# Roots of three group norms and attention's inverse denominators spread to all partitions through DRAM instead of by transposes on TensorE

## The chip, the cores and the metric

One core of a Trainium2 chip runs the whole program. The metric is the device time of one execution in microseconds (us), the median of several runs. The profile is that of one further execution. PE is TensorE, DVE VectorE, ACT ScalarE, POOL GpSimd; SP is SyncE, which only issues DMAs here.

## What is computed

One layer of a decoder trunk on 512 tokens of width 1024, in float32: an RMS norm, one large input projection, attention with dilated windows and a state-space branch (SSD, Mamba-2) side by side, a gated sum of both, an output projection, and a SwiGLU network. The two places of the change are the norm over each of four groups of 512 channels of the SSD branch, and the division by the softmax denominators of attention:

```python
# SSD branch: y (512 tokens, 2048), four groups of 512 channels
yg = (y * silu(z)).reshape(b, s, 4, 512)
yg = yg * rsqrt(mean(yg * yg, axis=-1, keepdims=True) + EPS)
# attention: per token and head, over three dilation groups
o = einsum('znhqk,znkhd->znqhd', p, vw) / den
attn = sum(softmax(lses) * outs)            # 8 heads of 64
```

## The kernel before

Tiles hold 128 channels on the partitions and the 512 tokens along the free dimension. Each weight chunk is a block of 1024 rows by 128 columns (512 KB, `wraw`), loaded by SP. ACT writes its upper part `whi` (L81) and DVE the rest `wlo` (L82), in a format with fewer bits, and PE takes three products per 128 rows: `whi` and `wlo` with the upper part of the data, `whi` with its lower part (`project`, L238; a chunk is 24 products of 512 columns). Each of `wraw`, `whi` and `wlo` has three buffers; loads run two chunks ahead and splits one.

Work of other kinds is threaded between the projections. `hook` (L223) is called in the middle and at the end of each projection; it runs what stands in `late`, moves each generator in `quick` on to its next `yield`, and at a projection's end moves the first generator in `slow` on. After that a scheduler orders the instructions of each engine; each engine then works through its own list in order, and waits where an instruction's semaphore is not there yet. In the SSD part PE, DVE and ACT are ordered by that scheduler too.

The SSD part goes through 16 blocks of 128 channels, four to a group. Each block takes two projections: one through a convolution (`acc`, `th`, `xf`, L525) and one for the gate `zs` (L676). `pair` (L547) then makes the block's decays `a` and `ce`, its states `S`, and `y`, with PE products of 64 rows (a with `xtm`, `ce` with `S`). After a group's last block, `group_end` (L601) takes sums of squares on PE, brings them to the power -1/2 on POOL (`gnr`, L273: token p of each 128 on partition p, four columns), and spreads them: `spread` (L283) transposes each column, repeated 128 times, against the identity on PE (four transposes, L182), so that every partition has the roots of all 512 tokens in PSUM. ACT copies them to `gnb` (L606), DVE multiplies the four `yg` by them (L610) and `split` makes `ssmh` and `ssml` (L258, L259). The second projection of these blocks (`ssm_half`, L617) takes blocks 0 to 7 in the first half, after the third group's blocks, and 8 to 15 much later.

Attention runs in four pairs of heads (`softmax_pair`, L717), each a generator in `slow`, its steps spread over the six projections that follow the pair's own. Small per-token numbers (maxima, `d0`, `d1n`) change their order of tokens by a trip through DRAM issued by POOL (L759 to L764, L781, L783). In the last step PE multiplies the exponentials with the values (`o0`, `o1`, 64-row products). `rd` (L814, L815) is the inverse denominator per token and head; POOL repeats it 64 times (L817), PE transposes that in four pieces into the PSUM bank `pr` (L820), and DVE multiplies the sum `t` of `o0` and `o1` by it (L824), after which `split` makes `ath` and `atl`, from which the merge (L925) takes its products.

Of the kernel before, what the change touches and what calls it, by code (L numbers as in the profile page):

```python
# [9 lines left out]
F32 = mybir.dt.float32  # L10
F32R = mybir.dt.float32r
AF = mybir.ActivationFunctionType
ALU = mybir.AluOpType

P = 128
S = 512
D = 1024
KD = D // P
NCH = S // P
# [149 lines left out]
def trunk(ctx: ExitStack, tc: tile.TileContext, xT, w_in, w_v, w_dt, w_attn, w_ssm, w_out, w_fi, w_fo,  # L169
          prm_d, relb_d, ident_d, tri_d, sid_d, oneh_d, outT, dbg=None):  # L170
    nc = tc.nc
    ev, act, gp, pe = nc.vector, nc.scalar, nc.gpsimd, nc.tensor

    def dump(name, t):
        if dbg and name in dbg:
            nc.gpsimd.dma_start(dbg[name], t)
# [4 lines left out]
    def turn(out, src):  # L181
        pe.transpose(out, src, ident)  # L182
# [10 lines left out]
    drm = ctx.enter_context(tc.tile_pool(name="drm", bufs=1, space=bass.MemoryType.DRAM))  # L193
# [3 lines left out]
    def bank(tag="aux"):  # L197
        cnt[0] += 1
        return psp.tile([P, S], F32, tag=tag, name=f"{tag}{cnt[0]}", bufs=4)
# [7 lines left out]
    def par(name, i=0, w=1):  # L207
        a = PRM[name][0]
        return prm[:, a + i : a + i + w]
# [44 lines left out]
    def split(pool, src, tag, i, tags=None):  # L254

        hi = pool.tile([P, S], F32R, tag=f"{tag}h{i}", name=f"{tag}h{i}_{cnt[0]}")
        lo = pool.tile([P, S], F32R, tag=f"{tag}l{i}", name=f"{tag}l{i}_{cnt[0]}")
        act.activation(hi, src, AF.Copy)  # L258
        ev.tensor_sub(lo, src, hi)  # L259
        return hi, lo  # L260

    def square_sums(ps, sq, first, last):

        for tt in range(sq.shape[1] // P):
            mm(ps[:, tt * 64 : tt * 64 + 64], sq[:, tt * P : tt * P + P], ones[:, :64], start=first and tt == 0, stop=last)

    def inv_root(pool, ps, nt, n, eps, tag):

        cnt[0] += 1
        v = pool.tile([P, NCH], F32, tag=f"{tag}v", name=f"{tag}v{cnt[0]}")[:, :nt]  # L270
        ev.tensor_scalar(v, ps[:, 0 : nt * 64 : 64], 1.0 / n, eps, op0=ALU.mult, op1=ALU.add)
        r = pool.tile([P, NCH], F32, tag=f"{tag}r", name=f"{tag}r{cnt[0]}")[:, :nt]
        gp.tensor_tensor(r, v, mhalf[:, :nt], ALU.pow)  # L273
        return r

    def mean_pow(pool, parts, n, eps, tag):

        ps = bank()
        for i, sq in enumerate(parts):
            square_sums(ps, sq, i == 0, i == len(parts) - 1)  # L280
        return inv_root(pool, ps, parts[0].shape[1] // P, n, eps, tag)

    def spread(r):  # L283

        pb = bank()
        for tt in range(r.shape[1]):
            turn(pb[:, tt * P : tt * P + P], r[:, tt : tt + 1].to_broadcast([P, P]))
        return pb
# [48 lines left out]
    dt, la, te, eE = [ssc.tile([P, P], F32, name=n) for n in ("dt", "la", "te", "eE")]  # L337
    relw = [drm.tile([HEADS, LREL[g]], F32, name=f"relw{g}") for g in range(3)]
    la_d = drm.tile([NSH, S], F32, name="la_d")
    h1_d = drm.tile([P, KD, S], F32, name="h1_d")  # L340
    v_d = [drm.tile([S, S], F32, name=f"v_d{g}") for g in range(3)]
    v_t = [v.rearrange("(c p) d -> p c d", p=P) for v in v_d]
# [6 lines left out]
    with tc.tile_pool(name="s0", bufs=1, reuse_waits="tile") as s0:  # L349
# [7 lines left out]
        v, ab, e, ri, ss, s2, h, dta = [s0.tile([P, P], F32, name=f"c{i}") for i in range(8)]  # L357
# [180 lines left out]
    with tc.tile_pool(name="sp", bufs=1, reuse_waits="tile") as sp:  # L538
# [8 lines left out]
        def pair(t, g, Bt, Cf, cbm, lab):  # L547
# [50 lines left out]
            if t % 4 == 3:  # L598
                quick[1].append(group_end(g))

        def group_end(g):  # L601
            r = mean_pow(sp, [yg.pop((g, "s"))], 512, 4.0 * EPS, "gn")
            yield
            pb = spread(r)
            rb = sp.tile([P, S], F32, tag="gnb", name=f"gnb{g}")
            act.activation(rb, pb, AF.Copy)  # L606
            yield
            for t in range(4 * g, 4 * g + 4):
                y = yg.pop(t)
                ev.scalar_tensor_tensor(y, y, par("nsw", t), rb, op0=ALU.mult, op1=ALU.mult)  # L610
                dump(f"ssm{t}", y)
                cnt[0] += 1
                ssm[t] = split(holder["ssm"], y, "ssm", t % 8)
                if t % 2:
                    yield
# [32 lines left out]
        for g in range(NG):  # L648
# [16 lines left out]
            for p in range(4):  # L665
                t = 4 * g + p
# [31 lines left out]
    attn = [None] * 4  # L698
    mscr = [drm.tile([S, 2], F32, name=f"mscr{i}") for i in range(4)]
    nscr = [drm.tile([S, 2], F32, name=f"nscr{i}") for i in range(4)]  # L700
    dscr = [drm.tile([S, 2], F32, name=f"dscr{i}") for i in range(4)]
    ahl_cm = tc.tile_pool(name="ahl", bufs=1, reuse_waits="tile", side="right")

    with tc.tile_pool(name="ap", bufs=1, reuse_waits="tile") as ap:

        def tl(shape, tag, name, bufs):
            return ap.tile(shape, F32, tag=tag, name=name, bufs=bufs)
# [9 lines left out]
        def softmax_pair(hp, q, k):  # L717
# [14 lines left out]
            for e in range(2):  # L732
                L0, T0 = Ls[e][0], Ts[e][0]
                pa, pb = bank(), bank()
# [78 lines left out]
            rd = tl([P, NCH, 2], "rd", f"rd_{hp}", 2)  # L813
            ev.tensor_add(rd, d0, d1n)  # L814
            ev.reciprocal(rd, rd)  # L815
            rdw = tl([P, NCH, P], "ot", f"rdw_{hp}", 2)
            gp.tensor_copy(rdw.rearrange("p b (e d) -> p b e d", e=2), rd.unsqueeze(3).to_broadcast([P, NCH, 2, 64]))  # L817
            pr = bank()
            for b in range(4):
                turn(pr[:, b * P : b * P + P], rdw[:, b])  # L820
            t = tl([P, S], "ot", f"ot{hp}", 2)
            act.activation(perm(t), regular(o1), AF.Copy)
            ev.tensor_add(t, t, o0)
            ev.tensor_mul(t, t, pr)  # L824
            dump(f"attn{hp}", t)
            attn[hp] = split(holder["ahl"], t, "at", hp)
            yield

        def ttr(out, ps, T, m):
            ev.tensor_tensor_reduce(out, ps, T, 1.0, -3.0e38, op0=ALU.add, op1=ALU.max, accum_out=m)  # L830
# [24 lines left out]
        halves = [slice(e * 64, e * 64 + 64) for e in range(2)]  # L855
# [43 lines left out]
        for hp in range(4):  # L899
            q, k = [], []  # L900
            for g in range(3):
                ps = project(bank("mm"), xn)
                q.append(class_queries(hp, g, ps) if g else first_queries(hp, ps))
                ps = project(bank("mm"), xn)
                k.append(class_keys(g, ps) if g else first_keys(hp, ps))
            slow.append(softmax_pair(hp, q, k))


        for j in range(KD):
            ps = project(bank("mm"), xn)  # L910
            t = tl([P, S], "ot", f"g1_{j}", 2)
# [42 lines left out]
    for i, j in enumerate(OUT_ORDER):  # L954
        t = tmp.tile([P, S], F32, tag="t", name=f"h1_{j}", bufs=2)
# [6 lines left out]
        p = j % 4  # L962
# [104 lines left out]
    for n in range(NF):  # L1067
# [7 lines left out]
        r, q, c1, c5 = heads.pop(n)  # L1075
# [5 lines left out]
        g = fp.tile([P, S], F32, tag="g", name=f"g{n}", bufs=2)  # L1081
# [46 lines left out]
    for j in range(KD - 1):  # L1128
# [6 lines left out]
        t = h1[j]  # L1135
# [175 lines left out]
```

## Time and profile before

| | |
|---|---|
| runs | 1148.74, 1148.74, 1149.55 us; median 1148.74 |
| the profiled execution | 1150.79 us |
| its span, from the first to the last instruction | 1149.0 us |
| mean granted clock of TensorE | 0.996 |
| SSD part, from the first to the fourth group's end | about 60 to 410 us |
| attention pairs | about 500 to 680 us |

In the rows below, times are in us and durations "mean ns of one" in ns. A row of the timeline reads: start, duration, engine, line, operation, output<-inputs, shapes, count, and in brackets the engine's idle time before it and what ended it. A row of waits reads: who waited, for whom, total us, times, longest. `mm` are the PSUM banks of the projections, `aux` those of all else; `PEld` is the loading of PE's stationary operand. In the list of DMA issues the last column is the median time from issue to landing. One `ce` with `S` or `a` with `xtm` counts as two instructions in the trace.

### The profile page before, as it was taken

Reading aid. Unit: us, or ns where it says so; the run is one execution under the profiler, and the core shown is the slowest. Engines: PE = TensorE matmul, PEld = TensorE weight load, DVE = VectorE, ACT = ScalarE, POOL = GpSimd, SP = SyncE. Lnnn points to the kernel's source line nnn. Section 1 sums busy time; section 2 is a strip of 40 time slices with the busy share of each in tenths; the row PEclk is TensorE's granted clock in tenths of the full one; section 3 lists DMA queues with packets and bytes.
Section 4 is the critical chain, followed back from the end, with each engine's and each line's share of the span. In section 5 each row is a group of like instructions: output and inputs, shape, how many; then the busy total and the mean of one; then the engine's idle time right before and its main releaser. Section 6 shows DMA issues by size and latency. Waiting matters only on the chain.

```text
span 1149.0 us, 17104 instructions
## 1 busy us (share of the span) xinstructions
PE 1132.8 (99%) x6636; PEld 969.5 (84%) x6636; DVE 715.3 (62%) x1253; ACT 569.9 (50%) x997; POOL 181.6 (16%) x169
## 2 busy tenths in 40 slices
PE   9999999999999999999999999999999999999996
PEld 6777888878888788888888888888999999988886
DVE  5777897873579333455564534478888777773222
ACT  5555565554345331336536533356767667663321
POOL 3214313222013300011211100000111111100001
PEclk9999999999999999999999999999999999999999
DMA  6343333233332373332333224345688888844322
GB/s 220 130 149 98 121 94 111 92 111 110 92 92 74 110 256 96 106 93 75 93 85 83 63 90 123 112 151 171 148 184 186 191 193 186 172 129 129 101 65 74
DMA packets 51521, 142.35 MB, mean 124 GB/s; under 512 B 6439, under 2 KB 13119, under 8 KB 51184
## 3 DMA queue, kind: packets, MB, share of 16 engines
q1 hardware_dynamic: 42096, 120.90, 33.9%
q0 software_dynamic: 6896, 16.04, 8.4%
q10 hardware_dynamic: 2448, 4.32, 1.3%
q8 instruction: 52, 0.85, 0.3%
q14 instruction: 29, 0.24, 0.1%
HBM read 133.76 MB, written 7.48 MB: 123 GB/s over the span
## 4 chain that ended last, share of the span: by engine, by line
PE 91%; DVE 4%; DMA 2%; ACT 1%; issue 1%; POOL 0%; SPq 0%; ACTq 0%; DVEq 0%; POOLq 0%
PE mm L179 74%; PE aux L179 15%; PE aux L182 2%; DVE wlo L82 1%; DMA x<-xT 0%; DMA lab<-la_d 0%; DVE frl L950 0%; DMA h_d<-h 0%; ACT whi L81 0%; DVE fS_lo L138 0%; DMA fa<-w_fi 0%; DVE xm L469 0%; DVE h L958 0%; POOL n2r L273 0%; DVE fA_lo L131 0%
## 5 line engine op out<-in xcount | busy, mean ns | idle before, releaser
L82 DVE TENSOR_TENSOR wlo<-wraw,whi 128x1024 fp32r<-128x1024 f32 (+2 forms) x156 | 185.7, 1195 | 185.3 <-ACT whi L81 185.1
L81 ACT ACTIVATE whi<-wraw 128x1024 fp32r<-128x1024 f32 (+2 forms) x156 | 152.2, 981 | 267.1 <-PE mm L179 238.1
L179 PE MATMUL mm<-xnh,whi 128*128 128x512 f32 x640 | 251.8, 393 | 1.4 <-DVE acc L530 1.3
L179 PE MATMUL mm<-xnh,wlo 128*128 128x512 f32 x640 | 252.6, 395 | 0.0
L179 PE MATMUL mm<-xnl,whi 128*128 128x512 f32 x640 | 251.1, 392 | 0.0
L179 PEld LDWEIGHTS mm<-xnh,whi 128*128 128x128 f32 x640 | 120.3, 188 | 27.3 <-ACT ce L562 1.7
L179 PEld LDWEIGHTS mm<-xnh,wlo 128*128 128x128 f32 x640 | 120.2, 188 | 26.9 <-issue 2.7
L179 PEld LDWEIGHTS mm<-xnl,whi 128*128 128x128 f32 x640 | 120.2, 188 | 24.9 <-issue 1.2
L179 PE MATMUL mm<-hhl,whi 128*128 128x512 f32 (+1 forms) x171 | 62.6, 366 | 0.6 <-DVE hhl L259 0.6
L179 PE MATMUL mm<-hhh,whi 128*128 128x512 f32 (+1 forms) x171 | 62.8, 368 | 0.2 <-ACT hhh L258 0.2
L179 PE MATMUL mm<-hhh,wlo 128*128 128x512 f32 (+1 forms) x171 | 62.3, 365 | 0.0
L121 POOL DMA_DIRECT2D fD_lo<-w_fi x22 | 19.1, 866 | 246.3 <-DVE h L958 135.8
L563 POOL TENSOR_TENSOR ce<-ce,Cf 128x768 f32<-128x768 f32 x16 | 34.7, 2173 | 140.9 <-ACT ce L562 78.2
L530 DVE SCALAR_TENSOR_TENSOR acc<-mm,hcw,acc 128x511 f32<-128x511 f32 (+2 forms) x72 | 53.2, 743 | 1.0
L138 DVE TENSOR_TENSOR fS_lo<-s,fS_hi 128x1024 fp32r<-128x1024 f32 x44 | 52.0, 1217 | 0.0
L179 PE MATMUL mm<-ssml,whi 128*128 128x512 f32 x128 | 50.2, 392 | 0.0
L179 PE MATMUL mm<-ssmh,wlo 128*128 128x512 f32 x128 | 50.1, 392 | 0.0
L179 PE MATMUL mm<-ssmh,whi 128*128 128x512 f32 x128 | 49.9, 390 | 0.0
L179 PE MATMUL mm<-frh,fS_hi 128*128 128x256 f32 x176 | 49.4, 281 | 0.5 <-ACT c L1031 0.5
L179 PE MATMUL aux<-frh,fS_hi 128*128 128x256 f32 x176 | 49.4, 280 | 0.0
L179 PE MATMUL aux<-frl,fS_hi 128*128 128x256 f32 x176 | 49.1, 279 | 0.0
L179 PE MATMUL aux<-frh,fS_lo 128*128 128x256 f32 x176 | 49.1, 279 | 0.0
(320 smaller groups left out, 2571.1 us busy)
## 6 DMA issues: line engine op xcount, KB each, us to landing
wraw<-w_in SPq DMA_DIRECT2D x80, 512.0 KB, 3.6
fb<-w_fi SPq DMA_DIRECT2D x22, 512.0 KB, 3.7
fa<-w_fi SPq DMA_DIRECT2D x22, 512.0 KB, 5.0
fA_lo<-w_fi POOLq DMA_DIRECT2D x19, 512.0 KB, 5.8
lab<-la_d SPq DMA_DIRECT2D x16, 512.0 KB, 3.7
wraw<-w_ssm SPq DMA_DIRECT2D x16, 512.0 KB, 3.8
wraw<-w_fo SPq DMA_DIRECT2D x15, 512.0 KB, 3.6
wraw<-w_v SPq DMA_DIRECT2D x11, 512.0 KB, 3.7
```

What stands on the lines that cost most here:

```text
L81: self.nc.scalar.activation(hi[:, cs], r[:, cs], AF.Copy)
L82: self.nc.vector.tensor_sub(lo[:, cs], r[:, cs], hi[:, cs])
L121: self.nc.gpsimd.dma_start(lo.rearrange("p (k n) -> p k n", n=P), src, accum_op=ALU.add)
L138: self.nc.vector.tensor_sub(lo, t, hi)
L179: pe.matmul(out, lhsT, rhs, start=start, stop=stop, skip_group_check=True)
L182: pe.transpose(out, src, ident)
L530: ev.scalar_tensor_tensor(acc[:, d:], ps[:, : S - d], hcw[:, t * 4 + 3 - d : t * 4 + 4 - d], acc[:, d:], op0=ALU.mult, op1=ALU.add)
L563: gp.tensor_mul(ce, ce, Cf[:, P:].unsqueeze(1).to_broadcast([P, 2, S - P]))
```

## The change

Two spreads leave PE.

In `group_end`, for the groups 0 to 2, SP writes the 128x4 roots to a row of 512 floats in DRAM (`gn_d`), token by token, and after that has landed reads the row into all 128 partitions (`gnb`, 256 KB). The four transposes and ACT's copy are gone there; the last group keeps them.

In `softmax_pair`, POOL's repetition, the four transposes and their PSUM bank are gone. SP writes `rd` in two pieces (one per head) to two rows in DRAM (`rscr`), and after a `yield` reads each row into 64 partitions (`rdw`, a tile of its own now). The multiplication and the split stand behind that `yield`, where the last step's `yield` was before; so they come one projection end later in the program, together with the next pair's first step.

```diff
+    gn_d = drm.tile([3, S], F32, name="gn_d")
...
         def group_end(g):
             r = mean_pow(sp, [yg.pop((g, "s"))], 512, 4.0 * EPS, "gn")
-            yield
-            pb = spread(r)
+            if g < 3:
+                nc.sync.dma_start(gn_d[g].rearrange("(c p) -> p c", p=P), r)
+            yield
             rb = sp.tile([P, S], F32, tag="gnb", name=f"gnb{g}")
-            act.activation(rb, pb, AF.Copy)
+            if g < 3:
+                nc.sync.dma_start(rb, gn_d[g : g + 1, :].partition_broadcast(P)[:, 0, :])
+            else:
+                act.activation(rb, spread(r), AF.Copy)
             yield
...
+    rscr = [drm.tile([2, S], F32, name=f"rscr{i}") for i in range(4)]
...
             ev.reciprocal(rd, rd)
-            rdw = tl([P, NCH, P], "ot", f"rdw_{hp}", 2)
-            gp.tensor_copy(rdw.rearrange("p b (e d) -> p b e d", e=2), rd.unsqueeze(3).to_broadcast([P, NCH, 2, 64]))
-            pr = bank()
-            for b in range(4):
-                turn(pr[:, b * P : b * P + P], rdw[:, b])
+            for e in range(2):
+                nc.sync.dma_start(rscr[hp][e].rearrange("(b p) -> p b", p=P), rd[:, :, e])
             t = tl([P, S], "ot", f"ot{hp}", 2)
             act.activation(perm(t), regular(o1), AF.Copy)
             ev.tensor_add(t, t, o0)
-            ev.tensor_mul(t, t, pr)
+            yield
+            rdw = tl([P, S], "rdw", f"rdw_{hp}", 1)
+            for e in range(2):
+                nc.sync.dma_start(rdw[halves[e], :], rscr[hp][e : e + 1, :].partition_broadcast(64)[:, 0, :])
+            ev.tensor_mul(t, t, rdw)
             attn[hp] = split(holder["ahl"], t, "at", hp)
-            yield
```

The lines of the changed kernel stand 1 to 6 further on: L606 and L610 become L611 and L615, the new DMAs are L605, L609, L823 and L830, and the multiplication of attention is L831.

On DVE, from the first group's mean of squares (`gnv44`) on, before the change; `yg0` to `yg3` are the group's blocks, `acc5` and `xf5` the convolution of block 5, `xw4` an operand of block 4's states:

```order
L271 TENSOR_SCALAR gnv44_1232<-aux43_1227 128x4
L660 TENSOR_TENSOR cbm1_1245<-aux46_1265,tri_81 128x512
L560 TENSOR_TENSOR a4_1391<-a4_1391,cbm1_1245 128x1024
L560 TENSOR_TENSOR a5_1528<-a5_1528,cbm1_1245 128x1024
L82 TENSOR_TENSOR wlo21_1511<-wraw21_1440,whi21_1510 128x1024
L530 SCALAR_TENSOR_TENSOR acc5_1427<-mm54_1370,hcw_82,acc5_1427 128x511
L530 SCALAR_TENSOR_TENSOR acc5_1427<-mm54_1370,hcw_82,acc5_1427 128x510
L610 SCALAR_TENSOR_TENSOR yg0_801<-yg0_801,prm_71,gnb0_1276 128x512
```

And the same place on DVE in the changed kernel, up to the end of what follows the multiplications directly:

```order
L271 TENSOR_SCALAR gnv44_1233<-aux43_1228 128x4
L665 TENSOR_TENSOR cbm1_1247<-aux46_1267,tri_81 128x512
L561 TENSOR_TENSOR a4_1388<-a4_1388,cbm1_1247 128x1024
L561 TENSOR_TENSOR a5_1525<-a5_1525,cbm1_1247 128x1024
L553 TENSOR_TENSOR xw4_1386<-xtm4_1306,te_87 128x384
L82 TENSOR_TENSOR wlo21_1508<-wraw21_1437,whi21_1507 128x1024
L615 SCALAR_TENSOR_TENSOR yg0_802<-yg0_802,prm_71,gnb0_1273 128x512
L615 SCALAR_TENSOR_TENSOR yg1_943<-yg1_943,prm_71,gnb0_1273 128x512
L615 SCALAR_TENSOR_TENSOR yg2_1081<-yg2_1081,prm_71,gnb0_1273 128x512
L615 SCALAR_TENSOR_TENSOR yg3_1210<-yg3_1210,prm_71,gnb0_1273 128x512
L531 SCALAR_TENSOR_TENSOR acc5_1424<-mm53_1367,hcw_82,acc5_1424 128x511
L259 TENSOR_TENSOR ssml0_47_1289<-yg0_802,ssmh0_47_1288 128x512
```

The convolution's `acc5` has moved behind the multiplications, and `xw4` ahead of them.

On PE, a stretch of block 5's 64-row products before the change (`mm64` is a projection of the time):

```order
L182 MATMUL aux62_1595<-ident_72,xf_6_1571 128x128 x4
L179 MATMUL aux63_1608<-a5_1528,xtm5_1436 64x128 x8
L179 MATMUL mm64_1645<-xnl6_418,whi22_1579 128x512
L179 MATMUL mm64_1645<-xnh6_417,wlo22_1580 128x512
L179 MATMUL mm64_1645<-xnh7_423,whi22_1579 128x512
L179 MATMUL aux63_1608<-ce5_1539,S5_1558 64x128 x4
L179 MATMUL mm64_1645<-xnl7_424,whi22_1579 128x512
L179 MATMUL aux63_1608<-ce5_1539,S5_1558 64x128
L179 MATMUL mm64_1645<-xnh7_423,wlo22_1580 128x512
L179 MATMUL aux63_1608<-ce5_1539,S5_1558 64x128
```

The same block's products of `ce5` with `S5` in the changed kernel stand at other seams, in three runs of two pairs, here the last two with what lies between:

```order
L179 MATMUL aux62_1605<-ce5_1536,S5_1555 64x128 x2
L179 MATMUL mm65_1711<-xnl7_425,whi23_1645 128x512
L179 MATMUL mm65_1711<-xnh7_424,wlo23_1646 128x512
L179 MATMUL mm68_1780<-xnh0_333,whi24_1714 128x512
L179 MATMUL mm68_1780<-xnl0_334,whi24_1714 128x512
L179 MATMUL aux62_1605<-ce5_1536,S5_1555 64x128 x2
```

Over blocks 4 to 11 such products stand in 18 separate runs before and in 16 after; elsewhere PE's list differs by the removed transposes alone.

On SP, at the first pair's inverse denominators in the changed kernel (`wraw82` to `wraw85` are weight chunks, which follow each other directly before the change):

```order
L65 DMA wraw82_4676<-w_in 128x1024
L823 DMA rscr0_3623<-rd_0_4663 128x4x1 x2
L830 DMA rdw_0_4706<-rscr0_3623 64x512
L65 DMA wraw83_4764<-w_in 128x1024
L830 DMA rdw_0_4706<-rscr0_3623 64x512
L65 DMA wraw84_4844<-w_in 128x1024
```

The two writes and the first read have come in ahead of chunk 83, and the second read behind it; the first read waits for the first write's landing, and chunk 83 stands behind that wait.

## The prediction

> **What bounds the kernel now.** I read the page first (busy times, the forty slices, the chain), then the sums over stretches, the waits of TensorE, and the timelines of the places that change. The page's first rows and two stretches (the second and third group of the SSD part, and the attention pairs):
>
> ```profile
> PE 1132.8 (99%) x6636; PEld 969.5 (84%) x6636; DVE 715.3 (62%) x1253; ACT 569.9 (50%) x997; POOL 181.6 (16%) x169
> ...
> 145.00:290.00 145.00, 145.00 (x840) 117.50 (x839) 108.95 (x203) 78.90 (x159) 36.20 (x22) 1.00 0.33 104
> ...
> 505.00:690.00 185.00, 185.00 (x1082) 156.42 (x1082) 92.90 (x226) 92.42 (x215) 23.25 (x34) 1.00 0.31 82
> ```
>
> In the second and third row the columns after the length are the busy time of PE, PEld, DVE, ACT and POOL. In both stretches PE has no idle time, at a granted clock of 1.00, while DVE is busy 75% and 50%. Busy could hide waits, so I look at when products start. PE's waits and the timeline around two removed spreads (the first stands alone between products, the second follows the attention's 64-row products):
>
> ```profile
> PE mm L179 <- DVE acc L530: 1.3, 1, 1.3
> ...
> 287.88 0.39 PE L179 MATMUL mm<-ssml,whi 128*128 128x512 f32 x1
> 288.11 0.60 PE L182 MATMUL aux<-ident,gnr 128*128 128x128 f32 x4
> 288.46 0.48 PE L179 MATMUL mm<-ssmh,wlo 128*128 128x512 f32 x1
> 288.78 0.39 PE L179 MATMUL mm<-ssmh,whi 128*128 128x512 f32 x1
> 289.01 0.39 PE L179 MATMUL mm<-ssml,whi 128*128 128x512 f32 x1
> ...
> 536.32 1.70 PE L179 MATMUL aux<-P,vt 128*64 128x128 f32 x28
> 537.95 0.66 PE L182 MATMUL aux<-ident,rdw 128*128 128x128 f32 x4
> 538.36 0.47 PE L179 MATMUL mm<-xnh,whi 128*128 128x512 f32 x1
> 538.67 0.39 PE L179 MATMUL mm<-xnl,whi 128*128 128x512 f32 x1
> ```
>
> Products of 512 columns start 0.23 us apart (288.78 to 289.01) although each takes 0.39: PE is an unbroken queue, and its longest wait in the SSD part is the row shown, and its rows have none in the attention. So what leaves PE's queue shortens the kernel, and what is only waited for elsewhere costs nothing until it holds up PE.
>
> **The change, part by part.** *Spreads that go.* Around the third group's spread, 287.88 to 288.78 is 0.90 us for one step from product to product, four transposes and a second step; without them two steps take 0.45. So a group's spread costs 0.45. Where the transposes of xf follow it, its share is the distance between their starts:
>
> ```profile
> 147.50 0.60 PE L182 MATMUL aux<-ident,gnr 128*128 128x128 f32 x4
> 147.94 0.60 PE L182 MATMUL aux<-ident,xf 128*128 128x128 f32 x4
> 148.29 0.47 PE L179 MATMUL mm<-xnh,wlo 128*128 128x512 f32 x1
> ```
>
> That is 0.44, so three group spreads are 1.3 us. For the attention, from the start of rdw's transposes (537.95) to the second product (538.67) is 0.72. Once they are gone, a product follows the 64-row products directly, and the step out of such a run costs what it costs in the SSD part:
>
> ```profile
> 93.47 0.39 PE L179 MATMUL mm<-xnl,whi 128*128 128x512 f32 x1
> 93.78 0.43 PE L179 MATMUL aux<-ce,S 128*64 128x128 f32 x2
> 94.15 0.50 PE L179 MATMUL mm<-xnh,wlo 128*128 128x512 f32 x1
> 94.48 0.39 PE L179 MATMUL mm<-xnh,whi 128*128 128x512 f32 x1
> ```
>
> 94.15 to 94.48 is 0.33, so 0.72 - 0.33 = 0.39 goes per pair, and four pairs are 1.6 us. The spreads sum to 2.9 us.
>
> One transpose by itself has a longer duration:
>
> ```profile
> L182 PE MATMUL aux<-ident,gnr 128*128 128x128 f32 x16 | 2.4, 272 | 0.0
> ```
>
> The mean is 272 ns, but they start a quarter of 0.44 us apart, and the sum goes by the starts. The Trainium skill (TensorE: Matmul & The Clock Gate, Part 4: PE-mode transpose) gives about 275 ns for a 128x128 transpose in a kernel's context; the trace's duration agrees, and by that figure 28 of them would be worth 7.7 us where the rows give 2.9.
>
> *Order of the rest.* The scheduler lays out blocks 4 to 11 of the SSD part anew (PE, DVE and ACT; before and behind them nothing moves but the edits). In the order of PE, the 64-row products of these blocks (a with xtm, ce with S) come in 18 separate runs before and 16 after. The last four rows price a run: 93.47 to 94.48 is 1.01 instead of two steps, 0.45, so 0.56 for one pair, while inside a long run a pair takes 2 x 1.63 / 28 = 0.12 (536.32 to 537.95). Joining a run to another saves 0.44; two fewer are 0.9 us. Bounds: 0, if other seams get dearer, and 1.8.
>
> *Copies.* ACT loses three copies of 0.6 us, POOL four of 1.04; both engines have idle time there, so I count nothing.
>
> *The trip at the groups.* The reader of gnb (L610, now L615) waits in DVE's queue for a write of 512 single floats and a read of 256 KB, one after the other, both issued from SP. The trace has no such pair; nearest are the maxima's small trips (512 pieces of 8 bytes, written and read) and loads of 256 KB:
>
> ```profile
> mscr<-m POOLq DMA_DIRECT2D x4, 4.0 KB, 4.6
> m1n<-nscr POOLq DMA_DIRECT2D x4, 4.0 KB, 2.3
> h<-xT ACTq DMA_DIRECT2D x8, 256.0 KB, 3.3
> x<-xT SPq DMA_DIRECT2D x8, 256.0 KB, 6.0
> ```
>
> The ends are 2.3 + 3.3 = 5.6 and 4.6 + 6.0 = 10.6 us; I take mscr, a write to DRAM like the new one, and h, loaded amid other traffic as gnb will be (x at the very start, with all queues full): 4.6 + 3.3 = 7.9. When does it hurt? The roots of the first two groups before, DVE around the first, and where PE stood at the second:
>
> ```profile
> 142.22 1.04 POOL L273 TENSOR_TENSOR gnr<-gnv,mhalf 128x4 f32<-128x4 f32 x1 [3.56 <-DVE gnv L271]
> 217.10 1.02 POOL L273 TENSOR_TENSOR gnr<-gnv,mhalf 128x4 f32<-128x4 f32 x1 [3.72 <-DVE gnv L271]
> ...
> 145.93 1.22 DVE L82 TENSOR_TENSOR wlo<-wraw,whi 128x1024 fp32r<-128x1024 f32 x1
> 147.07 1.52 DVE L530 SCALAR_TENSOR_TENSOR acc<-mm,hcw,acc 128x511 f32<-128x511 f32 x2
> 148.77 2.74 DVE L610 SCALAR_TENSOR_TENSOR yg<-yg,prm,gnb 128x512 f32<-128x512 f32 x4 [0.18 <-ACT gnb L606]
> 152.55 1.29 DVE L259 TENSOR_TENSOR ssml<-yg,ssmh 128x512 fp32r<-128x512 f32 x2
> ...
> 222.50 0.60 PE L182 MATMUL aux<-ident,gnr 128*128 128x128 f32 x4
> ```
>
> The roots are ready at 143.3, so the trip lands at about 151.2. DVE, which now has xw ahead of the multiplication in place of two acc, reaches it at about 147.7 and stands still some 3.5 us. Behind it, up to the convolution's xf5, stand the four multiplications (2.74), four acc (3.0), four ssml (2.6), two wlo (2.4), four narrow S (about 0.9, an estimate from their width beside ssml) and xf5 (0.7, like one ssml): 12.3. PE wants xf5 90 products later: it had 21 products between the scores (Cf with Bf) and 147.50, so the scores ended at 142.7; 90 x 0.227 = 20.4, and xw's products and xf4's transposes take another 1.1 (six steps and four steps of 0.11): 164.2. So the multiplication must start by 151.9, which allows a trip of 8.6 us. In the second group the scores ended 22 products ahead of 222.50, at 217.5; 61 products and the same 1.1 bring PE to xf6 at 232.5, ahead of it DVE has the multiplications, one wlo and xf6 (4.7), and from 218.1 on a trip of 9.7 is allowed. Behind the third group's multiplications stand only weights. For weights the cover is longer:
>
> ```profile
> ACT whi L81 <- PE mm L179: 238.1, 88, 5.9
> SPq L65 <- DVE wlo L82: 642.2, 135, 14.3
> ```
>
> ACT splits a chunk when PE releases a buffer, that is two chunks of 24 x 0.227 = 5.4 us ahead of use; less 1.1 for whi and 1.2 for wlo, 8.6 us remain for DVE to be late. SP likewise waits for buffers, not for transfers, so the 4 or 5 us that SP now stands between a write and its read, with the next weights queued behind, are covered too. At 7.9 us the trip costs nothing; at 10.6 it costs 2.0 + 0.9 = 2.9 us, at 5.6 nothing.
>
> *The trip of the attention.* It is issued from SP as soon as rd is there and read much later:
>
> ```profile
> L815 DVE RECIPROCAL rd<-rd x4: 203/203/205, 524.7 to 657.4; 128x8 f32<-128x8 f32 x4
> L824 DVE TENSOR_TENSOR ot<-ot,aux x4: 680/686/689, 540.1 to 675.0; 128x512 f32<-128x512 f32 x4
> L179 PE MATMUL mm<-ath,whi x32: 389/389/389, 689.4 to 748.5; 128*128 128x512 f32 x32
> ```
>
> Between rd and its use lie 15.4 us in the first pair and 17.6 in the last. The second read stands behind one load of weights in SP's queue, which waits for the wlo right behind rd, so even 10.6 us and that wait are in time; and the last pair's result is not wanted before 689.4. Nothing.
>
> **Sum.** -2.9 - 0.9 + 0 = -3.8 us. The profiled execution took 1150.79 (span 1149.0 and 1.8 around it), so it would become 1147.0. The runs' median of 1148.74 lies 2.05 below that execution; it becomes 1144.9, which is the forecast.
>
> **Rivals.**
>
> *A: the trip outlasts its cover a little.* At 10.6 us two waits give back 2.9, or the new order's seams give nothing: -0.9 to -2.9, so 1145.8 to 1147.8. For it: DVE is 75% busy there, and the two margins are 0.7 and 1.8 us. Against: the middle price fits.
>
> *B, slower: small writes crawl.* A 4 KB or 64 KB transfer can take far longer than its size when the queues are full:
>
> ```profile
> T<-relw SPq DMA_DIRECT2D x16, 64.0 KB, 4.3
> vt<-v_d SPq DMA_DIRECT2D x3, 1024.0 KB, 6.5
> ...
> DMA to landing us min/median/max: 2.9/4.0/9.2
> ```
>
> The last row is of those T loads: their longest, 9.2 us, come where they queue with vt's loads of 1 MB. If write and read take 9.2 each, the trip is 18.4: past 8.6 and 9.7 PE waits one for one, 9.8 + 8.7 = 18.5, and with -3.8 the time is 1163.4. It turns slower from a trip of about 11.1 us on (2.5 + 1.4 against 3.8). Against: no 1 MB load is under way at the groups.
> By the Trainium skill (DMA: Bandwidth & Descriptors, Rules for kernel authors) a pattern whose last dimension is not contiguous falls into one descriptor per element, and it advises against it; the rows with 512 pieces of 8 bytes, at 2.3 to 4.6 us, do not show that as ruin.
>
> *C: PE's full durations go.* If each transpose were worth its whole 0.272 us, 28 would be 7.6, and with the 0.9 of the order the time 1140.2. Against: the spacing.
>
> *D: no change.* If PE were paced by something else, such as weights, removal would only turn into waiting: 1148.7. Against: constant starts 0.23 apart and weights 8.6 us early.
>
> Chances: forecast 0.65, A 0.17, B 0.08, C 0.03, D 0.07. Under 0.2% (2.3 us, about what a measurement of this kernel can tell from no change) lies A's upper half and D. Faster 0.72, same 0.20, slower 0.08. The forecast's own range, with 0 and 1.8 for the order, is 1144.0 to 1145.8; the range reaches up through A and the runs' spread of 0.8 to 1148.2, and down 0.5 to 1143.5.
>
> **What would show it.** Right: PE's busy time falls by about 4 us with no new wait row above 1 us; L182 loses 28 transposes; DVE waits for DMA at L615, 3 to 4 us in the first group, and nothing at L831; the trip is 7 to 8 us. Wrong: new waits of PE for xf, S or wlo between 145 and 245 us, DVE waiting at L831, or a PE that loses products and keeps its time.

## The result, and the profile after

The change makes the kernel slower: 1157.62 us median against 1148.74, ratio 1.0074 (95% interval 1.0054 to 1.0094). The prediction was 1144.9, faster. One of the six runs of the changed kernel was slow from end to end (1602.19 us at a granted clock of 0.65) and stands outside the ratio. The profiled execution of the changed kernel took 1155.68 us (span 1153.9).

The page's first row, and the sums over the two stretches, now after:

```profile
PE 1130.0 (98%) x6608; PEld 965.1 (84%) x6608; DVE 718.8 (62%) x1253; ACT 568.3 (49%) x994; POOL 176.6 (15%) x165
```

```profile
145.00:290.00 145.00, 137.81 (x781) 110.25 (x780) 109.82 (x199) 73.80 (x146) 34.77 (x21) 0.98 0.32 102
505.00:690.00 185.00, 185.00 (x1081) 156.60 (x1080) 97.91 (x245) 93.37 (x215) 19.46 (x30) 1.00 0.33 86
```

The 28 transposes are gone (6636 to 6608), and in the attention stretch PE is as busy as before. In the SSD stretch PE, which had no idle time, now loses 7.2 us of 145, and its mean granted clock (the share of full speed at which TensorE was let run) falls to 0.98. PE's waits between 140 and 260 us, where it had none before:

```profile
PE aux L182 <- DVE xf L536: 3.8, 1, 3.8
PE mm L179 <- DVE acc L531: 3.2, 1, 3.2
```

Both are waits for DVE. The timeline of DVE at the first two groups, with the row that stands still and what follows it:

```profile
156.38 2.74 DVE L615 SCALAR_TENSOR_TENSOR yg<-yg,prm,gnb 128x512 f32<-128x512 f32 x4 [8.75 <-DMA gnb<-gn_d]
159.04 0.75 DVE L531 SCALAR_TENSOR_TENSOR acc<-mm,hcw,acc 128x511 f32<-128x511 f32 x1
...
164.28 0.75 DVE L531 SCALAR_TENSOR_TENSOR acc<-mm,hcw,acc 128x509 f32<-128x509 f32 x1
...
235.33 2.74 DVE L615 SCALAR_TENSOR_TENSOR yg<-yg,prm,gnb 128x512 f32<-128x512 f32 x4 [7.55 <-DMA gnb<-gn_d]
237.98 1.22 DVE L82 TENSOR_TENSOR wlo<-wraw,whi 128x1024 fp32r<-128x1024 f32 x1
239.12 0.69 DVE L536 SCALAR_TENSOR_TENSOR xf<-th,acc 128x512 f32<-128x512 f32 x1
```

DVE stands 8.75 and 7.55 us at the multiplication. Behind it stand, in the first group, the `acc` that gives the next projection its PSUM bank, in the second the `xf` that PE transposes. Why it stands so long is in the timeline of SP, in the view of the tile `gnr` (the DMA that leaves it is the write) and in the list of DMA issues, in this order:

```profile
143.31 0.38 SPq L605 DMA_DIRECT2D gn_d<-gnr  x1
152.10 0.33 SPq L609 DMA_DIRECT2D gnb<-gn_d  x1
```

```profile
DMA to landing us min/median/max: 8.1/8.3/8.8
```

```profile
rdw<-rscr SPq DMA_DIRECT2D x8, 128.0 KB, 4.5
gnb<-gn_d SPq DMA_DIRECT2D x3, 256.0 KB, 4.3
rscr<-rd SPq DMA_DIRECT2D x8, 2.0 KB, 9.6
gn_d<-gnr SPq DMA_DIRECT2D x3, 2.0 KB, 8.3
```

The read is issued when the write has landed, 8.8 us after its issue. The write of 2 KB takes longer than the read of 256 KB. With reads of 3.6 to 5.3 us the trips took 13.1, 11.7 and 13.7 us. PE's timeline around the first stall, and the sums over the 5 us behind each stall, show a second cost:

```profile
161.63 0.39 PE L179 MATMUL mm<-xnh,wlo 128*128 128x512 f32 x1
165.17 0.66 PE L179 MATMUL mm<-xnh,whi 128*128 128x512 f32 x1 [3.15 <-DVE acc L531]
165.63 0.63 PE L179 MATMUL mm<-xnl,whi 128*128 128x512 f32 x1
166.05 0.63 PE L179 MATMUL mm<-xnh,wlo 128*128 128x512 f32 x1
...
168.61 0.44 PE L179 MATMUL mm<-xnh,wlo 128*128 128x512 f32 x1
168.89 0.39 PE L179 MATMUL mm<-xnh,whi 128*128 128x512 f32 x1
```

```profile
165.00:170.00 5.00, 4.83 (x17) 3.79 (x19) 4.96 (x10) 2.13 (x4) 0.00 (x0) 0.66 0.52 189
240.00:245.00 5.00, 4.92 (x33) 3.78 (x34) 5.00 (x10) 2.25 (x9) 0.00 (x0) 0.66 0.30 108
```

From start to start the stall lasts 3.54 us (161.63 to 165.17), 3.3 more than a step. Then for 3.4 us products start 0.43 us apart in place of 0.23: the granted clock of these 5 us is 0.66. That is another 1.6 us; the second stall (4.0 us) is followed by a stretch of the same clock.

To separate the stages, I take PE's sums of squares (first of the first group, last of the fourth) and the merge's first product. Views of these tiles, before and then after:

```profile
L179 PE MATMUL aux<-ones,sqs x32: 217/275/275, 140.9 to 392.3; 128*128 128x64 f32 x32
L179 PE MATMUL mm<-ath,whi x32: 389/389/389, 689.4 to 748.5; 128*128 128x512 f32 x32
```

```profile
L179 PE MATMUL aux<-ones,sqs x32: 217/275/323, 141.0 to 401.7; 128*128 128x64 f32 x32
L179 PE MATMUL mm<-ath,whi x32: 388/390/390, 697.1 to 756.3; 128*128 128x512 f32 x32
```

The SSD stage grows from 251.4 to 260.7 us (+9.3); the stage from there to the merge, with the attention pairs in it, shrinks from 297.1 to 295.4 (-1.7). What comes ahead of and behind these stages differs by some us from one execution to another whatever the kernel (the first sums come at 136.7 to 141.0 us in the runs below), and in the profiled pair it hid part of the loss.

### The profile page after: what moved, and what is told of

The parts are those of the page before. It is cut to its first block, busy times and chain, and to the rows that moved or that the text cites. A ratio compares the mean times of both kernels' runs of the same rounds, so it can differ in the third digit from the quotient of the medians.

```text
span 1153.9 us, 17061 instructions
## 1 busy us (share of the span) xinstructions
PE 1130.0 (98%) x6608; PEld 965.1 (84%) x6608; DVE 718.8 (62%) x1253; ACT 568.3 (49%) x994; POOL 176.6 (15%) x165
## 4 chain that ended last, share of the span: by engine, by line
PE 83%; DVE 8%; DMA 5%; ACT 2%; issue 2%; POOL 1%; SPq 0%; ACTq 0%; DVEq 0%; POOLq 0%
PE mm L179 67%; PE aux L179 14%; PE aux L182 2%; DVE wlo L82 2%; DMA gn_d<-gnr 1%; DVE acc L531 1%; DMA h_d<-h 1%; ACT whi L81 1%; DMA gnb<-gn_d 1%; DVE a L559 0%; DVE fS_lo L138 0%; DMA x<-xT 0%; DVE yg L615 0%; DMA fb<-w_fi 0%; DVE frl L956 0%
## 5 line engine op out<-in xcount | busy, mean ns | idle before, releaser
L179 PE MATMUL mm<-frh,fS_lo 128*128 128x256 f32 x176 | 49.1, 279 | 0.0
```

What stands on the lines that cost most here:

```text
L179: pe.matmul(out, lhsT, rhs, start=start, stop=stop, skip_group_check=True)
```

## Experiments

Theory 1: the group trip is the whole loss. Its write takes nearly twice what I had priced, DVE stands in its queue at the multiplication, and PE runs out of work. Rivals: the attention's trips or SP's queue cost too; the scheduler's new order costs; SyncE's way of issuing small pieces is slow. The table has what was measured of the timed kernels, with stages from the two rows shown above (SSD stage, and from there to the merge). Each ratio is to runs of the kernel before that were taken beside it (medians of 1147.55 us for runs 1 to 4, 1148.71 for 5 to 7 and 1149.36 for 9).

| kernel | median us | ratio to before (95% interval) | SSD stage | to the merge | PE's waits near the groups, over 0.5 us |
|---|---|---|---|---|---|
| before, profiled | | | 251.4 | 297.1 | none |
| the change | 1157.62 | 1.0074 (1.0054 to 1.0094) | 260.7 | 295.4 | 3.2, 3.8 |
| 1 attention alone | 1146.49 | 0.9989 (0.9967 to 1.0011) | 251.4 | 295.4 | none |
| 2 groups alone | 1158.03 | 1.0092 (1.0073 to 1.0111) | 262.0 | 297.0 | 3.1, 4.7, 0.8 |
| 3 groups, 16-byte pieces | 1148.11 | 0.9998 (0.9983 to 1.0012) | 251.3 | 297.0 | 1.2 |
| 4 groups, write from POOL | 1159.51 | 1.0097 (1.0079 to 1.0115) | 261.9 | 297.1 | 3.7, 1.8, 1.3 |
| 5 attention and third group | 1146.12 | 0.9978 (0.9957 to 0.9998) | 250.9 | 295.4 | none |
| 6 both, 16-byte pieces | 1147.28 | 0.9988 (0.9966 to 1.0009) | 251.2 | 295.5 | 1.2 |
| 7 groups, later multiplication | 1162.31 | 1.0126 (1.0092 to 1.0161) | 265.9 | 297.1 | 5.1, 2.2, 1.1 |
| 9 all but the second group | 1146.46 | 0.9981 (0.9954 to 1.0007) | 251.0 | 295.5 | none |

**1. Attention alone.** `group_end` as before, the rest of the change as it is.

```diff
-            if g < 3:
-                nc.sync.dma_start(gn_d[g].rearrange("(c p) -> p c", p=P), r)
             yield
+            pb = spread(r)
...
+            act.activation(rb, pb, AF.Copy)
```

> Attention's inverse denominators go through DRAM, the three group norms keep their TensorE transposes. Theory 1 (the group trip is the whole loss): the attention trip is covered by other work, so this kernel is about 1.5 us faster than before, the four times 0.39 us of the removed transposes: a ratio near 0.9987. Theory 2 (the loss lies also in attention: the 8 to 11 us writes, or weights queued behind the trip on SyncE): slower than before by more than 2 us, with new PE waits in the attention stage.

The SSD stage is that of before to a tenth, and the stage to the merge is the shorter one of the change. The time as a whole cannot be told from no change, the stage can. The attention's writes are as slow here (the list of DMA issues), but nothing waits for them on PE:

```profile
rscr<-rd SPq DMA_DIRECT2D x8, 2.0 KB, 8.7
```

The attention's part does what it was predicted to do. The loss is not there.

**2. Groups alone.** `softmax_pair` as before, `group_end` as in the change; against the change:

```diff
-            for e in range(2):
-                nc.sync.dma_start(rscr[hp][e].rearrange("(b p) -> p b", p=P), rd[:, :, e])
...
+            pr = bank()
+            for b in range(4):
+                turn(pr[:, b * P : b * P + P], rdw[:, b])
...
```

> The three group norms go through DRAM, attention keeps its transposes. Theory 1: the loss is all here, and this kernel is slower than the whole change, by attention's 1.5 us: about 10 us over before, a ratio near 1.009, with PE waiting 3 to 4 us near 162 us and again near 236 us, and the group's write landing 8 to 9 us after its issue. Theory 2 (the loss lies also in attention): closer to before than the whole change is, under 6 us over it.

The SSD stage is 10.6 us longer, with the two PE waits of the change and a third of 0.8 us. All of the loss is here.

**3. The same with 16-byte pieces.** The root's row lies in DRAM so that a partition's four numbers are neighbours, and the multiplication undoes that by its views. The order of PE's work is that of run 2.

```diff
-                nc.sync.dma_start(gn_d[g].rearrange("(c p) -> p c", p=P), r)
+                nc.sync.dma_start(gn_d[g].rearrange("(p c) -> p c", c=NCH), r)
...
-                ev.scalar_tensor_tensor(y, y, par("nsw", t), rb, op0=ALU.mult, op1=ALU.mult)
+                    yv = y.rearrange("q (c p) -> q c p", p=P)
+                    ev.scalar_tensor_tensor(yv, yv, par("nsw", t), rb.rearrange("q (p c) -> q c p", c=NCH), op0=ALU.mult, op1=ALU.mult)
```

> As the run with the groups alone, with the same order of TensorE's work, but the root's row lies in DRAM so that each partition writes its four numbers as one piece of 16 bytes (128 pieces in place of 512 of 4 bytes); the multiplication reads the row through a strided view. Theory 1 (the number of pieces sets the write's time): the write lands in 2 to 4 us, the trip takes 6 to 8 us, the PE waits near 162 and 236 us are gone, and the kernel is 1 to 3 us faster than before. Rival (the new order of the work, or any trip at all, is what costs): still 6 us or more slower than before with PE idle in the first two groups.

The list of DMA issues, PE's waits between 140 and 260 us, and the view of the tile `gnb`, in this order:

```profile
gnb<-gn_d SPq DMA_DIRECT2D x3, 256.0 KB, 3.2
gn_d<-gnr SPq DMA_DIRECT2D x3, 2.0 KB, 2.1
```

```profile
PE aux L179 <- DVE S L574: 1.2, 1, 1.2
```

```profile
L617 DVE SCALAR_TENSOR_TENSOR yg<-yg,prm,gnb x12: 1130/1144/1172, 144.5 to 288.2; 128x512 f32<-128x512 f32 x12
```

The same 2 KB now take 2.1 us, and the 10.6 us are gone: the new order as such does not cost. But of the 1 to 3 us that I expected to gain only 0.1 came. One wait is left, in the second group, whose trip took 6.8 us: PE waits 1.2 us for the states `S`, which stand behind the multiplications and the `ssml`. The multiplications themselves are longer through the strided view, 1.14 us each for 0.75. For the four that is 1.6 us, more than the wait that is left, so this wait can come from the view as well as from the trip; no run parts the two. With the wait added back (its gap is 1.4 us more than a step) the stage gained 1.5 us, which is the three spreads' 1.3 and at most 0.2 for the order.

**4. The write issued by POOL.**

```diff
-                nc.sync.dma_start(gn_d[g].rearrange("(c p) -> p c", p=P), r)
+                nc.gpsimd.dma_start(gn_d[g].rearrange("(c p) -> p c", p=P), r)
```

> As the run with the groups alone, but the write of 512 single numbers is issued by GpSimd in place of SyncE. Theory 1 (the number of pieces sets the write's time, whoever issues it): it lands in 8 to 9 us again and the kernel stays 8 to 10 us slower than before. Rival (SyncE's own way of issuing many small pieces is slow): it lands in 2 to 5 us, as this kernel's rows of 8 bytes from GpSimd do, and the PE waits of the first two groups are gone, with a time within 3 us of before.

```profile
gnb<-gn_d SPq DMA_DIRECT2D x3, 256.0 KB, 5.2
gn_d<-gnr POOLq DMA_DIRECT2D x3, 2.0 KB, 8.2
```

Slow again, with the same loss (the SSD stage is 10.5 us longer): it is not who issues it. TensorE's order differs a little from run 2's (37 runs of 64-row products for 34), which doesn't touch the write's own time.

**5. Attention and the third group alone.** Both conditions of `group_end` in the change:

```diff
-            if g < 3:
+            if g == 2:
```

> The whole attention change, and of the groups only the third: groups 1 and 2 keep their transposes. TensorE's order is that of before but for the edits. Theory 1 (what costs is the groups' trip where something late in VectorE's queue is wanted by TensorE; behind the third group stand only weights): the attention gives 1.64 us as in the run with attention alone, the third group 0.47 us, no new PE wait over 1 us: 2.1 us faster than before, a ratio near 0.998. Rival (any trip at a group costs): PE waits near 300 us and the kernel is no faster than with attention alone.

The third group's trip took 13.2 us (a write of 7.5, a read of 5.7), no shorter than those that cost so much, and DVE stood for it just as long:

```profile
284.56 1.23 DVE L82 TENSOR_TENSOR wlo<-wraw,whi 128x1024 fp32r<-128x1024 f32 x1 [3.98 <-ACT whi L81]
294.94 2.74 DVE L615 SCALAR_TENSOR_TENSOR yg<-yg,prm,gnb 128x512 f32<-128x512 f32 x4 [9.16 <-DMA gnb<-gn_d]
297.60 2.35 DVE L82 TENSOR_TENSOR wlo<-wraw,whi 128x1024 fp32r<-128x1024 f32 x2
```

Yet PE lost nothing: only weights stand behind it, and those are early. The stage is 0.5 us shorter, as priced for one spread. This kernel is faster than the one before and than the change: 0.9978 of before, with an interval (0.9957 to 0.9998) that just leaves out no change.

**6. The whole change with 16-byte pieces.** The groups are as in run 3. In attention DVE first copies `rd` into partition order, and one write takes both heads (the multiplication's view changes with it).

```diff
-            for e in range(2):
-                nc.sync.dma_start(rscr[hp][e].rearrange("(b p) -> p b", p=P), rd[:, :, e])
+            rdt = tl([P, 2, NCH], "rdt", f"rdt_{hp}", 2)
+            ev.tensor_copy(rdt.rearrange("p e b -> p b e"), rd)
+            nc.sync.dma_start(rscr[hp].rearrange("e (p b) -> p e b", b=NCH), rdt)
```

> The whole change, with 16-byte pieces in all writes (in attention rd is first put into partition order by one more copy on VectorE, and the multiplications read the rows through strided views). Theory 1: the attention gives its 1.64 us, the SSD part stands about where it stood before (0.14 us less in the run of the groups alone with 16-byte pieces, after its one PE wait of 1.3 us): 1.8 us faster than before, a ratio near 0.9985, and 11 us faster than the whole change with 4-byte pieces. Rival (SyncE's queue or the number of trips costs): 3 us or more slower than before.

```profile
gnb<-gn_d SPq DMA_DIRECT2D x3, 256.0 KB, 3.5
rscr<-rdt SPq DMA_DIRECT2D x4, 4.0 KB, 2.7
gn_d<-gnr SPq DMA_DIRECT2D x3, 2.0 KB, 1.9
```

The stages are the sum of runs 1 and 3: 0.2 and 1.6 us shorter than before. Ten us lie between this and the change, and they go with the form of the writes.

**7. The multiplication later in DVE's queue.** The write is the slow one. `holder["last"]` is the latest `xf` instruction, behind which the multiplication is now issued.

```diff
+            if g < 3:
+                for _ in range(5):
+                    yield
+            last = holder["last"]
...
-                ev.scalar_tensor_tensor(y, y, par("nsw", t), rb, op0=ALU.mult, op1=ALU.mult)
+                with tc.issue_after(last.ins):
+                    ev.scalar_tensor_tensor(y, y, par("nsw", t), rb, op0=ALU.mult, op1=ALU.mult)
```

> As the run with the groups alone, its slow write of 512 single numbers included, but the multiplication that waits for the row is put later in VectorE's queue, behind the convolution's last acc and xf of the next block (five more steps of the scheduler and an issue-after). TensorE's order changes too: 38 runs of 64-row products in place of 36 before and 34 in the groups-alone run. Theory 1 (VectorE standing still in order ahead of work that TensorE wants is what costs): the trip still takes 12 to 13 us and VectorE still waits, but the PE waits for acc and xf of 3 to 5 us are gone, and the SSD part takes no more than 2 us more than before. Rival (the trip or its queueing delays TensorE in another way, through weights or DMA): it stays 6 us or more over before.

A miss: the waits for `acc` and `xf` are gone, but the stage is 14.5 us longer. Timelines of DVE, ACT and PE in the second group, in this order:

```profile
224.77 0.68 DVE L536 SCALAR_TENSOR_TENSOR xf<-th,acc 128x512 f32<-128x512 f32 x1
235.13 2.74 DVE L620 SCALAR_TENSOR_TENSOR yg<-yg,prm,gnb 128x512 f32<-128x512 f32 x4 [9.67 <-DMA gnb<-gn_d]
```

```profile
235.91 2.62 ACT L258 ACTIVATE ssmh<-yg 128x512 fp32r<-128x512 f32 x4 [9.81 <-DVE yg L620]
238.43 0.26 ACT L570 ACTIVATE S<-aux 128x128 f32<-128x128 f32 x1
```

```profile
238.75 0.69 PE L179 MATMUL aux<-ce,S 128*64 128x128 f32 x4 [5.06 <-ACT S L570]
```

`xf` is now done ahead of the wait, but ACT stands too: its splits `ssmh` wait for the multiplication, and behind them stands the copy of `S` that PE wants next. So theory 1 was too narrow in naming DVE. A late row stops every queue that has one of its readers in it, or a reader of what they make, as ACT's splits here, and taking the first waiter out of the way uncovers the next.

**8 and 10. What makes the write slow.** Before, with chained writes to a DRAM tile at its end; each starts when the one ahead of it has landed. `src` is a tile of the kernel and `q` its first four columns; the first three lines are from run 8, the last two from run 10.

```diff
+        nc.sync.dma_start(prb_d[0, 0:512].rearrange("(c p) -> p c", p=P), q)
+        nc.sync.dma_start(prb_d[0, 0:512].rearrange("(p c) -> p c", c=4), q)
+        nc.sync.dma_start(prb_d[0, 0:1024].rearrange("(c p e) -> p c e", p=P, e=2), src[:, 0:8].rearrange("p (c e) -> p c e", e=2))
...
+        for e in (1, 2, 4, 8, 16):
+            nc.sync.dma_start(prb_d[0, 0:512 * e].rearrange("(c p e) -> p c e", p=P, e=e)[:, :, 0], src[:, 0:4])
...
```

> The kernel before, with writes of small pieces to one DRAM tile added at its end on SyncE, each waiting for the one ahead of it, all sent twice: 512 pieces of 4 bytes side by side in DRAM in the order of the change (neighbours come from different partitions), 128 of 16 bytes, 512 of 8 bytes, 512 of 4 bytes at a pitch of 8 bytes, the same with a partition's pieces next to each other, 512 of 4 bytes at a pitch of 64 bytes, 128 of 4 bytes, 256 of 4 bytes. Theory 1a (the time goes by the number of pieces): all of 512 pieces take 8 us, 256 some 5, and both of 128 some 2 to 3. Theory 1b (pieces of 4 bytes side by side from different partitions hinder each other): 512 of 4 bytes side by side take 8 us, but 512 of 8 bytes about 4.6, as the maxima's rows did, and those at 64 bytes pitch clearly less than 8. Theory 1c (any piece under 8 bytes is slow by itself): all rows of 512 of 4 bytes take 8 whatever their pitch, those of 8 bytes 4.6.

> The kernel before, with chained writes of small pieces to one DRAM tile at its end, all in the order in which neighbours come from different partitions, sent twice: 512 pieces of 4 bytes at pitches of 4, 8, 16, 32 and 64 bytes, then 512 pieces of 8, 16, 32 and 64 bytes side by side, then 32 pieces of 4 bytes from 32 partitions, then 128 pieces of 4 bytes from 16 partitions with 8 each. If the time goes by how many pieces fall into one stretch of 64 bytes (16 at 4 bytes: 9 us; 8: 4; 1: 2, from the first probe): pitch 16 takes some 2.5 to 3 us, pitch 32 some 2.2, 64 some 2; pieces of 16 and 32 bytes side by side the same as pitch 16 and 32; the last two rows 7 us again, though they have 32 and 128 pieces. If the time goes by the number of pieces instead: all rows of 512 pieces take the same whatever the pitch, and 32 pieces take 2 us.

SP's timeline of run 8; the distance between starts is the time of a write. L1207 is the write of the change, L1208 has 128 pieces of 16 bytes, L1209 512 of 8 bytes, L1210 and L1212 512 of 4 bytes at a pitch of 8 and 64, L1211 those of L1210 in an order in which a partition's four lie next to each other, L1213 only 128 of 4 bytes side by side, L1214 256:

```profile
1136.17 0.64 SPq L1207 DMA_DIRECT2D prb_d<-h1a  x1
1145.12 0.34 SPq L1208 DMA_DIRECT2D prb_d<-h1a  x1
1147.52 0.36 SPq L1209 DMA_DIRECT2D prb_d<-h1a  x1
1151.65 0.36 SPq L1210 DMA_DIRECT2D prb_d<-h1a  x1
...
1155.47 0.60 SPq L1211 DMA_DIRECT2D prb_d<-h1a  x1
...
1159.97 0.37 SPq L1212 DMA_DIRECT2D prb_d<-h1a  x1
1162.15 0.34 SPq L1213 DMA_DIRECT2D prb_d<-h1a  x1
1169.26 0.36 SPq L1214 DMA_DIRECT2D prb_d<-h1a  x1
1178.14 0.36 SPq L1207 DMA_DIRECT2D prb_d<-h1a  x1
```

That is 9.0 us for 512 single floats side by side, 2.4 in 16-byte pieces, 4.1 in 8-byte pieces, and 2.2 for the same 512 single floats 64 bytes apart; but 7.1 for only 128 of them side by side. At a pitch of 8 bytes the order of the partitions brings nothing: L1211 took 4.5 us in both passes, L1210 3.8 and 4.0. Run 10, from issue to landing, in both passes:

| 512 pieces, distance of neighbours | 4 B | 8 B | 16 B | 32 B | 64 B |
|---|---|---|---|---|---|
| single floats at that pitch, us | 9.7, 10.1 | 4.6, 4.8 | 2.7, 3.1 | 1.9, 2.5 | 1.8, 1.9 |
| pieces of that size, side by side, us | | 4.7, 4.5 | 2.9, 3.0 | 1.7, 1.7 | 1.7, 1.8 |

For 512 pieces the time goes by their distance, and their number alone doesn't set it: one expectation of theory 1 (run 3 was to be fast because it has fewer pieces) was right for a wrong reason. The last two rows of run 10 missed in part: 128 pieces from 16 partitions took 8.6 and 8.7 us, more than the 7 expected, but 32 pieces took 3.1 to 3.3 and not 7. So side by side the number counts too: 3.1 to 3.3 us for 32 single floats, 7.1 to 7.4 for 128, 8.7 to 8.9 for 256 and 8.9 to 9.4 for 512 in run 8. The wait comes after the DMA engines: in the second pass of run 8 all 528 packet records of the side-by-side write (issued at 1178.1) lie between 1179.0 and 1179.5 us, and no DMA engine is busy from there to the landing 8 us later; for the write at 64 bytes they take the same 0.5 us, and it lands within 0.5 us more. What behind the engines makes neighbours wait for each other these runs don't show.

**9. All but the second group.** The first and third group with the 16-byte pieces of run 3; the second, with the least room, as before. Against run 6 (attention's writes, not shown, are those of the change):

```diff
-            if g < 3:
+            if g in (0, 2):
```

> The whole attention change, and groups 1 and 3 through DRAM with 16-byte pieces (strided reads in the multiplication); the second group, whose trip had the least room, keeps its transposes. TensorE's order: 38 runs of 64-row products, 36 before. Theory 1 (a trip below the room that VectorE's queue has costs nothing, and the room at the first group is about 8 us with the longer strided multiplications): no PE wait over 1 us, each of the two groups gives 0.4 to 0.5 us, attention 1.64, together 2.5 us, a ratio near 0.998, with 0.4 us either way for the order. Rival (the order or the strided multiplications cost as much as the spreads): no better than attention with the third group alone.

A miss: the stage is 0.4 us shorter, not 0.9, no better than with the third group alone, though no wait is over 0.4 us. The rival holds: what the first group's spread gives is taken back. PE waits for nothing new, so what remains is the order of its own products (38 runs of 64 rows for 36); that is argued and not shown, for no run tries that order by itself.

## Why the prediction was wrong, point by point

- **What bounds the kernel: right.** PE is an unbroken queue; each us that it waits is lost, and DVE's 9 us at the third group cost nothing.
- **Spreads, 2.9 us: right** where a run shows them alone. Attention gives 1.6 to 1.7 (runs 6 and 1), the third group 0.5 (run 5). The first two groups come out as priced only in run 3, with its wait added back; in run 9 the first gave nothing. The transposes' durations (rival C) would have given 7.6.
- **Order of the rest, -0.9: wrong.** Run 3, with two runs of 64-row products fewer, gained at most 0.2 beside the spreads; run 9, with two more, came out 0.5 short of its two spreads, where the price was 0.9. A count of runs did not price an order here.
- **Copies, nothing: right.**
- **The trip at the groups, 7.9 us and no cost: this is the step that failed.** The trips took 13.1, 11.7 and 13.7 us, and the first two made PE wait. I took the write's 4.6 us from the row of the maxima, 512 pieces of 8 bytes, as nearest to 512 pieces of 4 bytes. It took 8.1 to 8.8. The row was near in the number of pieces and half as crowded, and run 10 prices just that: 4.6 against 9.7 us. I had put 10.6 us as the upper end by a read of 6.0; the reads were within my rows (3.6 to 5.3), the write was not.
- **The room that the trip has: about right as a size, wrong in its waiters.** I allowed 8.6 us in the first group and 9.7 in the second. Trip less stall gives 13.1 - 3.3 = 9.8 and 11.7 - 4.0 = 7.7. In the first group PE did not wait for xf5 but, earlier, for a PSUM bank that `acc` frees; in the second, DVE took up the mean of squares 2.2 us after PE had finished the sums (222.32 after 220.13 us; before the change 0.2 us), so the trip began late. Run 3 uncovered `S`, run 7 ACT's queue. With a write of 4.6 the trip would have been near this room; with the 8.8 and 8.1 measured it is past it in both groups.
- **What a stall costs: missed.** In the change each of the two stalls drew about 3.4 us at near half the rate behind it, 1.6 and 1.9 us more. That is no fixed price: run 2's first stall, 3.1 us without a product like the change's 3.15, was followed by full rate, and its second, of 4.7 us, by nearly 5 us of half clock. So: 3.3 + 1.6 + 4.0 + 1.9 - 1.3 = 9.5 for the SSD stage; measured 9.3.
- **The trip of the attention, nothing: right**, in spite of writes of 9.6 us. DVE waited 1.0 us once at the multiplication, where I had said not at all; PE did not wait.
- **Rivals.** B, small writes crawl, is what happened: the turning point I gave, a trip of 11.1 us, lies below the measured 11.7 to 13.7, and the trip was nearer to that than to B's 18.4. I gave it 0.08 because no large loads were under way; but the writes crawl at the quiet end of the program as well (runs 8 and 10), for their own form. I had left aside the rule of the Trainium skill (DMA: Bandwidth & Descriptors, Rules for kernel authors) against patterns with a last dimension that is not contiguous, because the maxima's rows did not bear it out. Its advice was right here, and the trace bears out a descriptor per element (528 packet records for 512 floats); but their count does not set the time (512 single floats 64 bytes apart take 1.8 us, 128 side by side 7.1).

## What to carry to other kernels

A row of the trace prices a small transfer only if it has the same pieces at the same distance: 512 single floats written side by side as pieces of their own take twice as long as pairs and three to four times as long as pieces of 16 bytes, so lay such a row out by partition, where a partition's numbers make one piece, and undo that where it is read (here at 0.4 us more for each multiplication). A trip off the critical path is not free for being long hidden: list every queue that holds one of its readers (here DVE's multiplication and ACT's split), and for each what stands behind the reader and when PE wants it. Take the trip where only early work stands behind it, as at the third group and in the attention, and leave TensorE's few tenths where not.

## What the runs showed of the hardware

- Writes of small pieces to DRAM: 512 single floats take 8.9 to 10.1 us side by side, 3.8 to 4.8 at a pitch of 8 bytes, 2.7 to 3.1 at 16, and 1.8 to 2.2 at 64, in runs 8 and 10; issued from SP or POOL alike (8.8 and 8.2 at the groups).
- TensorE's clock after a stall. In the change, products start 0.43 us apart for 3.4 us behind 3.15 us without a product (granted clock 0.66). Behind run 3's 1.2 us nothing is seen (granted 1.00 throughout), but 2.2 us in run 7, up to 185.7, were enough, while 3.1 us in run 2, from 159.2 to 162.3, were not. The length of a stall alone doesn't tell. Sums over two stretches of run 7, then one of run 2:

```profile
180.00:185.00 5.00, 3.45 (x32) 2.22 (x30) 5.00 (x4) 4.01 (x13) 3.01 (x2) 1.00 0.27 108
185.00:190.00 5.00, 4.32 (x12) 2.37 (x13) 3.95 (x15) 0.72 (x1) 0.00 (x0) 0.57 0.30 107
...
165.00:170.00 5.00, 4.97 (x45) 4.13 (x45) 4.96 (x10) 2.91 (x11) 0.00 (x0) 1.00 0.42 122
```

The Trainium skill (TensorE: Matmul & The Clock Gate, Part 1: The HAM clock gate) has the clock halve after at least one idle window of about 3.4 us. The 0.43 us between products, nearly twice the 0.23, agree with a halved clock. The idle time does not: both 3.15 and 2.2 us, behind which the clock fell, are shorter than that window.
